# One layer of a pooling and sparse-attention trunk: the first gates computed as block products with seven multiplications

## The chip, the cores and the metric

The kernel runs on one core of a Trainium2 chip. A core has five engines with a queue each: PE (TensorE) multiplies matrices into PSUM, DVE (VectorE) and ACT (ScalarE) do elementwise work on SBUF and PSUM, POOL (GpSimd) does elementwise work on SBUF alone, and SP (SyncE) issues most DMAs. An engine works through its own queue in order and waits on semaphores for the others. The metric is the device time of one execution in microseconds (us). Before the change three runs gave 812.95, 813.62 and 814.96 us, median 813.62.

## The reference, cut to what matters

One layer (DEPTH = 1) on 512 tokens of width 1024, all in float32:

```python
h = rms_norm(x, norm_mix[l])
proj = h @ w_in[l]
u, q, kc, vc, ksl, vsl, kwn, vwn, g_nsa, g_merge = jnp.split(proj, IN_SPLITS, axis=-1)
y_pool = pool_mixer(u, w_pool[l], pool_scale[l])
y_nsa = nsa_mixer(q, kc, vc, ksl, vsl, kwn, vwn, g_nsa, ...)
g_a, g_b = jnp.split(jax.nn.sigmoid(g_merge), 2, axis=-1)
merged = g_a * (y_pool @ w_proj_pool[l]) + g_b * (y_nsa @ w_proj_nsa[l])
x = x + merged @ w_out[l]
h = rms_norm(x, norm_mlp[l])
x = x + jnp.square(jax.nn.relu(h @ w_ff1[l])) @ w_ff2[l]
return rms_norm(x, norm_final)
```

The change concerns `g_a`, "the first gates": columns 2352 to 3375 of `w_in` (1024 columns, in a projection of 1024 inputs by 512 tokens), and their sigmoid.

## The kernel before, in words

**Precision.** PE reads its operands in a reduced float32 (`FR`). Each float32 operand is therefore split into a high part (a copy rounded to `FR`, made by ACT) and a low part (the value minus the high part, made by DVE or POOL), and a product is made of three matmuls: high by high, high by low, low by high (`split_products`, line 396). The tokens' halves are `R1` and `R2` (`hT`), features on partitions, eight blocks of 128 by 512 tokens. A weight tile of 1024 columns is loaded by SP into one of four buffers with the tag "raw" (`emit_load`, line 216) and split by `emit_prep_half` (line 321, in two halves of 512) or `group_steps` (line 289, whole). Split weights go to a ring of two buffers ("wh", "wl"); some keys have a place of their own in `dest`, as the compression weights `wk`, `wv` have in `wkt`.

**Stages.** First the norm: rows of `x` are scaled and turned in four blocks of 128 tokens, and their halves written to `R1` and `R2` (`sums0`, `turn0`, `evac0`, lines 534 to 560). Then P1 (list at line 125, loop from line 853): all projections that must stand before the attention starts, in the order of the list. `fm` (line 462) makes one block of 128 output columns for all 512 tokens: 24 matmuls of 512 columns (eight k blocks by three), then a "post" step evacuates the PSUM bank. P1 makes the keys (`ck`, `ks`, `kw`), the values (`V0` to `V2`), the pooling inputs (`u0` to `u3`, mixed by `pool_mix` on DVE, line 790), the compression of keys and values (`wk`, `wv`, lines 707 and 722), the first three query blocks (`q0` to `q2`, with `rope`, line 612), the eight blocks of first gates (`ga0` to `ga7`, line 869: a sigmoid into `MA`), four small pooling products (`pool_out`, line 839), and the pooling projection (`pp0` to `pp3`, line 875), which multiplies `MA`. Stage P2 runs the attention with the remaining projections (`FILL2`: the second gates `gb` and `q3` to `q7`) as filler; then come the output projection and the MLP.

**The seven-product algorithm.** The MLP already uses it (class `Group`, line 1362, and `product`, line 1344). A weight of 1024 by 512 is taken as four blocks of 512 by 256, the input as four blocks of 512 features by 256 tokens. In place of eight block products it makes seven, of sums and differences of blocks: `A11`, `S3`, `S1`, `S2`, `A12`, `A22`, `S4`. A product is 24 matmuls of 256 columns. The sums of weight blocks are made on DVE or by DMA, the sums of tokens (`T1` to `T4`) on DVE, and each sum is split into high and low again. The results are put together in PSUM and on DVE (`main`, `last`): `A12` adds to the bank of `A11`, `A22` to that of `S3` after DVE has read it, `S4` to that of `S1` after DVE has read it (`NEEDS`).

**Places.** `GB` (4096 columns of float32) is the second gates' place in P2 and scratch in P1 (`cmp_first`, `pool_mix`). `oT` is the attention's output in P2 and scratch in P1 (`pool_mix`, `cmp_rest`, small weights). `MA` holds the first gates and is unused until `ga0`.

**Order.** The program text sets which work follows which by generators ("side") and by `ahead`, which prepares weights up to three keys ahead. The order in which instructions stand in each engine's queue is then fixed by the framework's scheduler when the program is built; it moves independent instructions past each other.

Of the kernel before, what the change touches and what calls it, by code (L numbers as in the profile page):

```python
# [62 lines left out]
def trunk(ctx: ExitStack, tc: tile.TileContext, A, out):  # L63
# [22 lines left out]
    GB = cp.tile([128, 8, S], F32, name="GB")  # L86
    GBf = GB.rearrange("p j t -> p (j t)")

# [16 lines left out]
    def add_key(k):  # L105
# [14 lines left out]
        else:  # L120
# [4 lines left out]
    P1 = ("ck ks u0 wk0 wk1 u1 wk2 u2 kw wk3 cv V0 V1 V2 wv0 u3 wv1 q0 wv2 wpool ga0 ga1 wv3 ga2 q1 "  # L125
          "ga3 ga4 ga5 q2 ga6 ga7 pp0 pp1 pp2 pp3").split()
    FILL2 = "gb0 q3 q4 q5 gb1 gb2 q6 gb3 q7 gb4 gb5 gb6 gb7".split()
    for k in P1 + FILL2:
        add_key(k)
# [8 lines left out]
    IN_TURN = ("A11", "S3", "S1", "S2", "A12", "A22", "S4")  # L138
# [77 lines left out]
    def emit_load():  # L216
# [22 lines left out]
        if i >= len(P1) + len(FILL2) + 4 and (len(begun) > 2 or begun and st["sums"] == len(jobs)):  # L239
            add_sum()  # L240
        return True

    def sums_after(i):

        if i < MLP0:
            return len(P1) + 3 <= i < len(P1) + len(FILL2) + 8
        return i % 3 == 0
# [72 lines left out]

    def emit_prep_half():
# [4 lines left out]
        if WL[i][0][0] in "AS":  # L326
            if "gen" not in part:
                part["gen"] = group_steps(i)
# [97 lines left out]

    hT = (R1, R2)
# [52 lines left out]
    oT = op.tile([128, 8, S], F32, name="oT")  # L480
    oTf = oT.rearrange("p j t -> p (j t)")
# [10 lines left out]
    rows = oTf[0:36, 2080:2208]  # L492
    w2 = {kv: oTf[:, 2208 + 128 * i:2336 + 128 * i].rearrange("p (k c) -> p k c", k=2) for i, kv in enumerate("kv")}
# [174 lines left out]
    with ExitStack() as c1:  # L668
# [9 lines left out]
        for k in P1:  # L678
            if k[:2] in ("wk", "wv"):
                dest[k] = wkt + ["wkt"]  # L680

        def cmp_first(kv):

            def post(ps):
                kc = GBf[:, 0:1024].rearrange("p (g t) -> p g t", g=2)
# [3 lines left out]
                a = GBf[:, 1024:2048].rearrange("p (j n) -> p j n", j=16)  # L689
# [32 lines left out]
        def cmp_rest(kv, ps):  # L722
            t = oTf[0:64, 1056:2080].rearrange("p (a n) -> p a n", a=4)
# [27 lines left out]
            pm = ps1.tile([128, 2, 64], F32, tag="M", bufs=2, name="psM")  # L751
            if kv == "k":
# [31 lines left out]
        POOL.memset(GBf[:, 2560:2576], 0.0)  # L784
        POOL.memset(GBf[:, 3088:3104], 0.0)
        yd = [p1.tile([128, 4, S], FR, name=f"yd{e}") for e in range(2)]

        mixing = []

        def pool_mix(g):  # L790
            def post(ps):
# [3 lines left out]
                u = oTf[:, 528 * (g % 2):528 * (g % 2) + 528]  # L795
# [5 lines left out]
                while sh < w:  # L801
                    nx = GBf[:, 2560 + 528 * (sh % 3 - 1):2560 + 528 * (sh % 3)]
# [4 lines left out]
                d = GBf[:, 2048:2560]  # L807
# [6 lines left out]
                mixing.clear()  # L814
            return post
# [30 lines left out]

        first_posts += [cmp_first("k"), lambda ps: rope(ps, -0.125, k_done(0))]
# [5 lines left out]
        for k in P1[2:]:  # L853
            i = int(k[-1]) if k[-1].isdigit() else None
            if k == "kw":
# [28 lines left out]
    OT = hT  # L884

# [4 lines left out]
    with ExitStack() as c2:  # L890
# [27 lines left out]
        def split_ready():  # L918

            while free and ready:  # L920
                p, half = ready.pop(0)
                c = slice(256 * half, 256 * half + 256)
                ACT.activation(OT[0][:, p, c], oT[:, p, c], AF.Copy)
                DVE.tensor_tensor(OT[1][:, p, c], oT[:, p, c], OT[0][:, p, c].bitcast(F32), op=ALU.subtract)
# [189 lines left out]
        def o_evac(p, half):  # L1114
# [3 lines left out]
            for h in range(2):  # L1118
                DVE.tensor_tensor(oT[64 * h:64 * h + 64, p, 256 * half:256 * half + 256].rearrange(
# [116 lines left out]
    MAf = MA.rearrange("p j t -> p (j t)")  # L1236

    def quarter(f, i):
        return f[:, 1024 * i:1024 * i + 1024].rearrange("p (k t) -> p k t", k=4)

# [96 lines left out]
    def pair(f, i):  # L1337
        return f[:, 512 * i:512 * i + 512]

# [3 lines left out]

    def product(ps, key, first, mm):

        w, n = use(key), 0
        for f in range(2):
            for k in range(4):
                for u, v in ((0, 0), (0, 1), (1, 0)):
                    mm(ps[:, 256 * f:256 * f + 256], w, f, k, u, v, start=first and n == 0, stop=n == 23,  # L1350
                       skip_group_check=True)
                    n += 1
                    if n % 6 == 0:
                        ahead()
                        step_side()

    def until(ready):
        while not ready():
            assert side
            step_side()  # L1360

    class Group:

        def __init__(self, c, g, Y):
            self.c, self.g, self.Y = c, g, Y
            self.s = pair(GBf, 6 + g)
            self.u2, self.u3, self.c21 = pair(MAf, 6 + g), pair(MAf, 0), pair(MAf, 1)
            self.ps, self.done = {}, set()  # L1370

        def pe(self, o):
            key = f"{o}1{self.c}{self.g}"
            until(lambda: o not in self.NEEDS or self.NEEDS[o] in self.done)
            if not self.done:
                side.append(self.main())
            name, x, *at = self.X[o]

            def mm(out, w, f, k, u, v, **kw):
                PE.matmul(out, w[u][:, k, 128 * f:128 * f + 128], XB[x][v][:, k, :], **kw)  # L1380
            if not at:
                self.ps[name] = bank()
# [270 lines left out]
```

## Time and profile before

| | us |
|---|---|
| three runs | 812.95, 813.62, 814.96 |
| the profiled execution's own time | 811.65 |
| its span | 809.8 |
| busy: PE, DVE, ACT, POOL | 788.0, 621.4, 491.3, 207.9 |
| first `fm` of P1 after the keys (`u0`) starts | 26.1 |
| last `pp` result multiplied | 170.1 |

The mean granted PE clock is 0.996 of full speed. The span is the time from the first to the last instruction on the core, the execution's own time adds what lies around it. In the rows, an instruction's duration includes its latency, so that matmuls and DVE instructions that follow each other without a wait overlap a little: the distance from start to start is what one costs in a queue that is never empty.

### The profile page before, as it was taken

To read this page: it belongs to the slowest core of one execution; us is meant where nothing else is said; L and a number is where in the kernel's file an instruction comes from. 1 tells how busy PE (TensorE), PEld (TensorE's weight loads), DVE (VectorE), ACT (ScalarE), POOL (GpSimd) and SP (SyncE) were. 2 spreads that over 40 slices of the span, in tenths; PEclk is the share of its full clock that TensorE was granted. 3 is DMA by queue.
4 is the path that set the end of the run, shared out by engine and by line. 5 is a ranking of instruction groups with operands and counts; after the bars stand their busy time and mean duration, and the time that the engine had idled before them with its cause. 6 is when DMAs were issued, how large, how long until landed. Compare 5 with 4: busy or idle time off the path is not lost.

```text
span 809.8 us, 14149 instructions
## 1 busy us (share of the span) xinstructions
PE 788.0 (97%) x5163; PEld 709.1 (88%) x5163; DVE 621.4 (77%) x1217; ACT 491.3 (61%) x968; POOL 207.9 (26%) x273
## 2 busy tenths in 40 slices
PE   8999999998999999999999999999999999999996
PEld 7889878887788888888788899999999999999996
DVE  5796744547888888888664579996899689978975
ACT  6576533327878788899434476934773477347833
POOL 4000000028777867674334100111111110000000
PEclk9999999999999999999999999999999999999999
DMA  9554632357456524554954807999899997754522
GB/s 306 141 161 120 167 92 92 104 162 164 66 134 136 129 72 93 104 132 93 313 146 155 203 2 217 317 242 284 243 285 225 286 262 207 211 165 156 185 76 105
DMA packets 128752, 136.65 MB, mean 169 GB/s; under 512 B 5349, under 2 KB 117001, under 8 KB 128522
## 3 DMA queue, kind: packets, MB, share of 16 engines
q1 hardware_dynamic: 107274, 113.98, 43.3%
q0 software_dynamic: 21120, 20.97, 18.2%
q8 instruction: 41, 0.67, 0.3%
q10 hardware_dynamic: 288, 0.79, 0.3%
q14 instruction: 29, 0.24, 0.1%
HBM read 131.01 MB, written 44.04 MB: 216 GB/s over the span
## 4 chain that ended last, share of the span: by engine, by line
PE 75%; DVE 14%; ACT 5%; issue 3%; POOL 2%; DMA 1%; SPq 0%; ACTq 0%; DVEq 0%; POOLq 0%
PE psF L394 22%; PE psB L1380 15%; PE psB L394 12%; PE psB L1499 9%; PE psO L1110 3%; PE psT L1076 3%; PE psS L1014 3%; DVE wl L308 2%; PE psV L394 2%; PE psF L451 1%; DVE w3l L308 1%; PE psC L714 1%; DVE P L1036 1%; ACT wh L306 1%; POOL P L1059 1%
## 5 line engine op out<-in xcount | busy, mean ns | idle before, releaser
L394 PE MATMUL psF<-R,wh 128*128 128x512 f32 x512 | 166.6, 404 | 0.8 <-ACT GB L688 0.6
L306 ACT ACTIVATE wh<-raw 128x1024 fp32r<-128x1024 f32 x70 | 74.0, 1058 | 74.0 <-PE psB L1499 32.6
L351 ACT ACTIVATE wh<-raw 128x512 fp32r<-128x512 f32 (+1 forms) x100 | 60.1, 620 | 82.5 <-PE psF L394 38.2
L394 PEld LDWEIGHTS psF<-R,wh 128*128 128x128 f32 x512 | 92.4, 189 | 19.0 <-ACT GB L688 0.9
L273 POOL DMA_DIRECT2D S<-w_ff x40 | 46.4, 1160 | 233.1 <-DMA S<-w_ff 163.5
L394 PE MATMUL psF<-R,wl 128*128 128x512 f32 x256 | 101.9, 398 | 0.4 <-DVE wl L353 0.4
L308 DVE TENSOR_TENSOR wl<-raw,wh 128x1024 fp32r<-128x1024 f32 x70 | 85.3, 1219 | 16.8 <-ACT wh L306 16.7
L1059 POOL TENSOR_SCALAR P<-P,sm,GT 128x128 f32<-128x128 f32 (+3 forms) x128 | 86.0, 708 | 42.2 <-DVE sm L1056 28.7
L353 DVE TENSOR_TENSOR wl<-raw,wh 128x512 fp32r<-128x512 f32 (+1 forms) x74 | 53.5, 734 | 33.3 <-ACT wh L351 32.3
L1046 ACT ACTIVATE P<-P,sm 128x128 f32<-128x128 f32 (+3 forms) x128 | 71.0, 556 | 9.5 <-DVE sm L1036 8.5
L1036 DVE CUSTOM_DVE_ANT_0 P<-psS,cst 128x128 f32<-128x128 f32 (+3 forms) x128 | 59.7, 484 | 6.8 <-PE psT L1076 5.1
L1380 PE MATMUL psB<-R,wh 128*128 128x256 f32 x352 | 64.1, 282 | 0.0
L1087 ACT ACTIVATE PT<-psT 128x512 fp32r<-128x512 f32 (+2 forms) x96 | 49.5, 520 | 19.7 <-PE psT L1076 19.0
L353 POOL TENSOR_TENSOR wl<-raw,wh 128x512 fp32r<-128x512 f32 x28 | 38.1, 1364 | 88.4 <-ACT wh L351 86.1
L306 ACT ACTIVATE w3h<-raw 128x1024 fp32r<-128x1024 f32 x35 | 37.0, 1056 | 39.2 <-PE psB L1499 17.0
L1091 DVE TENSOR_TENSOR PT<-psT,PT 128x512 fp32r<-128x512 f32 (+2 forms) x96 | 56.5, 594 | 3.4 <-ACT PT L1087 2.6
L394 PEld LDWEIGHTS psF<-R,wl 128*128 128x128 f32 x256 | 48.3, 189 | 11.4 <-DVE wl L353 0.6
L1076 PE MATMUL psT<-ident,P 128*128 128x128 f32 x320 | 51.6, 275 | 4.8 <-POOL P L1059 4.0
L1380 PEld LDWEIGHTS psB<-R,wh 128*128 128x128 f32 x352 | 54.1, 189 | 0.3 <-DVE R L1322 0.2
L308 DVE TENSOR_TENSOR w3l<-raw,w3h 128x1024 fp32r<-128x1024 f32 x35 | 42.7, 1220 | 14.4 <-ACT w3h L306 14.4
L1076 PEld LDWEIGHTS psT<-ident,P 128*128 128x128 f32 x320 | 40.0, 142 | 14.7 <-POOL P L1059 6.9
L1380 PE MATMUL psB<-R,wl 128*128 128x256 f32 x176 | 49.5, 281 | 0.0
(385 smaller groups left out, 2295.7 us busy)
## 6 DMA issues: line engine op xcount, KB each, us to landing
raw<-w_ff SPq DMA_DIRECT2D x55, 512.0 KB, 5.2
S<-w_ff POOLq DMA_DIRECT2D x40, 512.0 KB, 7.7
raw<-S SPq DMA_DIRECT2D x40, 512.0 KB, 4.4
raw<-w_in SPq DMA_DIRECT2D x32, 512.0 KB, 3.9
S<-w_ff SPq DMA_DIRECT2D x30, 512.0 KB, 5.4
S<-S SPq DMA_DIRECT2D x10, 512.0 KB, 6.2
raw<-w_proj_nsa SPq DMA_DIRECT2D x8, 512.0 KB, 4.2
raw<-w_out SPq DMA_DIRECT2D x8, 512.0 KB, 3.5
```

The lines of the kernel that those rows point to most:

```text
L306: ACT.activation(h, t, AF.Copy)
L308: DVE.tensor_tensor(l, t, h.bitcast(F32), op=ALU.subtract)
L351: ACT.activation(h[:, sl], t[:, sl], AF.Copy)
L353: eng.tensor_tensor(l[:, sl], t[:, sl], h[:, sl].bitcast(F32), op=ALU.subtract)
L394: PE.matmul(ps, a, b, start=first and j == 0, stop=last and j == n - 1, skip_group_check=True)
L1036: DVE.tensor_tensor_reduce(out=P[:, o:o + n].rearrange("p (a c) -> p a c", c=128), in0=s, in1=m, scale=1.0, scalar=3e38, op0=ALU.add, op1= ...
L1046: last_exp[:] = [ACT.activation(c, c, AF.Exp, bias=sm[:, 0, e:e + 1], scale=-1.0, accum_out=sm[:, 1, e:e + 1])]
L1059: r = POOL.tensor_scalar(P[:, o:o + n], P[:, o:o + n], sm[:, 2, e:e + 1], GT[:, qb, c + e:c + e + 1], op0=ALU.mult, op1=ALU.mult)
L1076: PE.transpose(pt[:, 128 * j:128 * j + 128], P[:, 128 * j:128 * j + 128], ident)
L1091: DVE.tensor_tensor(dL, src, dH.bitcast(F32), op=ALU.subtract)
L1380: PE.matmul(out, w[u][:, k, 128 * f:128 * f + 128], XB[x][v][:, k, :], **kw)
L1499: PE.matmul(out, YB[y][u][:, k, 128 * f:128 * f + 128], w[v][:, k, :], **kw)
```

## The change

The eight blocks `ga0` to `ga7` (8 by 24 matmuls of 512 columns) become two groups `GA0` and `GA1` of 512 gate columns each, every group made by the class `Group` with seven products of 24 matmuls of 256 columns. `product`, `until` and `Group` move up in the file and take their bank, operands and places as arguments; the MLP calls them with the old ones.

- *Weights*: per group four blocks of 512 by 256 are loaded into the four "raw" buffers (`add_gates`), and their sums made in place by DVE (`gate_steps`). Each of the fourteen operands is split whole (1024 columns). `S1` and `A22` use the place of the compression weights (`wkt`), the other five the ring.
- *Tokens*: `token_sums` adds the halves of `R1` and `R2` back to float32 in `MA`, makes `T1` to `T4` on DVE, and splits each. `T3` and `T1` lie in the place of `GB`, once pooling's four mixings no longer use it as scratch, `T2` and `T4` in the two halves of the place of `oT`.
- *Order of P1*: `q0` and `q1` move ahead of the gates, `u3` behind `q0`, all four `wv` and `wpool` ahead of `GA0`; `q2` stands between the groups. The four `pool_out` stand behind the first four products of `GA0`.
- `GB` and `oT` are allocated after P1 in the same places; `oT` in two tiles.

```diff
-    P1 = ("ck ks u0 wk0 wk1 u1 wk2 u2 kw wk3 cv V0 V1 V2 wv0 u3 wv1 q0 wv2 wpool ga0 ga1 wv3 ga2 q1 "
-          "ga3 ga4 ga5 q2 ga6 ga7 pp0 pp1 pp2 pp3").split()
+    P1 = ("ck ks u0 wk0 wk1 u1 wk2 u2 kw wk3 cv V0 V1 V2 wv0 q0 wv1 u3 wv2 q1 wv3 wpool GA0 q2 GA1 "
+          "pp0 pp1 pp2 pp3").split()
...
+    def add_gates(g):
+        at = {b: len(LD) + n for n, b in enumerate(("21", "11", "22", "12"))}
+        for b in at:
+            i, j, c = int(b[0]) - 1, int(b[1]) - 1, 2352 + 512 * g
+            w = w_in[512 * j:512 * j + 512, c + 256 * i:c + 256 * i + 256]
+            LD.append([(w.rearrange("(k p) c -> p k c", p=128), 0)])
+        gate_loads.append(at)
+        WL.extend((f"{o}G{g}", None) for o in IN_TURN)
...
+    def gate_steps(i):
+        o, g = WL[i][0][:-2], int(WL[i][0][-1])
+        if o == "A11":
+            kept.clear()
+        for b in {"A11": ("11",), "S3": ("21",), "S1": ("22",), "A12": ("12",)}.get(o, ()):
+            while st["load"] <= gate_loads[g][b]:
+                assert emit_load()
+            kept[b] = raws.pop(gate_loads[g][b])[0]
+        h, l = dest[WL[i][0]][:2] if WL[i][0] in dest else slot_of(i)
+        to, b = {"S3": ("11", "21"), "S1": ("21", "22"), "S2": ("11", "22")}.get(o, ("12" if o == "S4" else o[1:], None))
+        t = kept[to]
+        if b:
+            DVE.tensor_tensor(t, t, kept[b], op=ALU.add)
+            yield
+        ACT.activation(h, t, AF.Copy)
+        yield
+        DVE.tensor_tensor(l, t, h.bitcast(F32), op=ALU.subtract)
...
+        if o == "A12":
+            yield
+            DVE.tensor_tensor(t, t, kept["11"], op=ALU.add)
+        if o in ("S1", "A12", "A22", "S4"):
+            emit_load()
...
+        def token_sums():
...
+            def sum_of(o, to, a=None, b=None, alu=None):
+                if alu:
+                    DVE.tensor_tensor(to, a, b, op=alu)
+                    yield
+                if o == "T3":
+                    made[:] = flat(cp.tile([128, 8, S], FR, tag="GB", bufs=1, name="TS"))
+                elif o != "T1":
+                    made[:] = flat(op.tile([128, 4, S], FR, tag=f"oT{o == 'T2':d}", bufs=1, name="TS"))
+                h, l = (made.pop(0) for _ in range(2))
+                ACT.activation(h, to, AF.Copy)
+                yield
+                DVE.tensor_tensor(l, to, h.bitcast(F32), op=ALU.subtract)
...
+            for b in ("11", "12", "22", "21"):
+                whole(b)
+                yield
+            while len(mixed) < 4:
+                yield
+            DVE.tensor_tensor(x["11"], x["11"], x["12"], op=ALU.subtract)
+            yield from sum_of("T3", x["12"], x["22"], x["12"], ALU.subtract)
+            yield from sum_of("T1", x["11"])
+            yield from sum_of("T2", x["11"], x["22"], x["11"], ALU.add)
...
+            yield from sum_of("T4", x["21"], x["11"], x["21"], ALU.subtract)
...
-            elif k[:2] == "ga":
-                def post(ps, j=i):
-                    ACT.activation(MA[:, j, :], ps, AF.Sigmoid)
-                run(fm(k, ps1, post))
-                if i < 4:
-                    pool_out(i)
+            elif k[:2] == "GA":
...
+                group = gates(i)
+                for n, o in enumerate(IN_TURN):
+                    group.pe(o)
+                    if i == 0 and n < 4:
+                        pool_out(n)
```

`Group`'s steps on DVE, as in the MLP:

```python
DVE.tensor_tensor(self.u2, self.s, self.ps["b"], op=ALU.subtract)
DVE.tensor_tensor(self.u3, self.ps["c"], self.u2, op=ALU.add)
self.done.add("u3")
yield
DVE.tensor_tensor(self.u3, self.ps["d"], self.u3, op=ALU.add)
self.done.add("u2")
```

More of the change, by code (lines that the diff above doesn't have):

```diff
@@ new lines, in gates, with act @@
+        def gates(g):
+            def act(src, f, th):
+                yield
+                ACT.activation(MA[:, 4 * g + 2 * f:4 * g + 2 * f + 2, 256 * th:256 * th + 256],
+                               src.rearrange("p (f t) -> p f t", f=2), AF.Sigmoid, scale=-1.0 if f else 1.0)
+            own = [pair(gate_f[0], i) for i in range(4)]
+            at = own[1:] + own[:1] if g else [own[0], pair(MAf, 6), pair(MAf, 7), pair(MAf, 4)]
+            return Group(f"G{g}", sums_of.get, lambda: ps1.tile([128, S], F32, tag="V", bufs=4, name="psV"), at, act)
```

218 lines of the change are left out of this document (128 added, 90 removed).

## The prediction

> **What bounds the kernel now.** I began with the page: the busy times, and the chain that ended last.
>
> ```profile
> span 809.8 us, 14149 instructions
> PE 788.0 (97%) x5163; PEld 709.1 (88%) x5163; DVE 621.4 (77%) x1217; ACT 491.3 (61%) x968; POOL 207.9 (26%) x273
> PE 75%; DVE 14%; ACT 5%; issue 3%; POOL 2%; DMA 1%; SPq 0%; ACTq 0%; DVEq 0%; POOLq 0%
> ```
>
> PE is the bound over the whole, DVE the second. What a change in P1 is worth has to be read in P1, so I asked for the busy time by stretches (columns: length, then PE, weight load, DVE, ACT, POOL busy, the granted clock, DMA).
>
> ```profile
> 20.00:40.00 20.00, 19.35 (x116) 16.81 (x115) 15.29 (x27) 11.63 (x22) 0.16 (x1) 1.00 0.50 140
> 40.00:60.00 20.00, 20.00 (x99) 16.73 (x98) 18.07 (x40) 13.97 (x27) 0.00 (x0) 1.00 0.59 168
> 60.00:86.00 26.00, 26.00 (x159) 23.59 (x158) 19.23 (x39) 15.01 (x34) 0.00 (x0) 1.00 0.47 130
> 86.00:127.00 41.00, 40.80 (x185) 32.61 (x184) 24.32 (x52) 18.54 (x35) 1.39 (x4) 1.00 0.43 118
> 127.00:170.00 43.00, 43.00 (x189) 35.12 (x188) 18.12 (x31) 11.79 (x22) 0.29 (x1) 1.00 0.41 119
> 195.40:199.50 4.10, 4.10 (x19) 3.51 (x19) 2.46 (x11) 2.28 (x6) 2.65 (x4) 0.62 0.70 160
> ```
>
> From 40 to 170 us PE never stops. DVE is nearly full from 40 to 60 and about 60% and 42% busy in the stretches where the gates are made. So PE's work counts there, as long as DVE's stays below it. The last row is used further down. The chain in order of time gives PE's prices:
>
> ```profile
> 73.05 0.95 PE psC L714 x8
> 74.00 5.60 PE psF L394 x24
> 80.55 5.59 PE psF L394 x24
> 120.14 51.35 PE psF L394 x222
> 171.49 0.81 PE psC L950 x8
> ...
> 499.96 10.26 PE psB L1380 x86
> 540.27 17.38 PE psB L1499 x144
> ```
>
> A matmul of 512 columns costs 51.35/222 = 0.2313 us, one of 256 columns 10.26/86 = 0.1193 (0.1207 in the last row).
>
> **The saving on PE.** Removed are 8 x 24 = 192 matmuls of 512 columns: 44.4 us. Added are 14 x 24 = 336 of 256 columns: 40.1 us. The saving is 4.3 us (3.8 at the dearer price). A block product less in eight saves 12.5% of the columns, but the narrow matmul costs 3% more per column.
>
> **What DVE gets.** Prices, start to start in a full queue:
>
> ```profile
> 518.85 1.14 DVE wl L308
> 519.98 0.60 DVE yT3L L1439
> 537.17 1.22 DVE raw L317
> 538.39 1.13 DVE w3l L308
> ...
> 118.46 0.76 DVE L626 TENSOR_TENSOR rx<-rx,cst 128x256 f32<-128x256 f32 x2 [2.77 <-DMA rs<-rx]
> 119.14 0.76 DVE L629 TENSOR_TENSOR rs<-rs,cst 128x256 f32<-128x256 f32 x2
> 123.28 0.20 DVE L777 TENSOR_TENSOR VC<-psM,VC 32x64 fp32r<-32x64 f32 x1
> ```
>
> 1024 columns cost 1.14, 512 columns 0.60 to 0.69 (I take 0.62), 256 columns (119.14 - 118.46)/2 = 0.34, a tiny one 0.2. Removed are 16 subtractions of 512 columns, 9.9 us. Added are 14 subtractions and 8 weight sums of 1024 (25.1 us), four whole tokens, four sums and four subtractions of 1024 (13.7 us), and ten steps of the groups of 512 (6.2 us): 45.0 us, net 35 us more on DVE over P1. That would fit into P1's idle time if it were spread out. The changed program's queue shows that it isn't: the whole tokens and two sums are placed before 35 us, but the other two sums and all four splits need places that pooling's last mixing (`u3`) or the value compression still holds, and so stand behind `u3`.
>
> So I follow DVE's queue from there. In the old order the second full block after the values ends at 80.55 + 5.59 = 86.14; in the new one it is `u3`. With the start's delay of 0.4 (below) it ends at 86.5, ACT's copy takes 0.58:
>
> ```profile
> 80.61 0.58 ACT L797 ACTIVATE oT<-psF 128x512 f32<-128x512 f32 x1
> ```
>
> and DVE starts `u3`'s first running sum at 87.1. From it up to the step that frees the bank of `S1` for `S4` in the first group (the last of `main`) the queue holds, in its built order, 17 instructions of 1024 columns (four sums and seven low parts of weights; low parts of T3, T1, T2, T4 and the sums for T2 and T4), 19 of 512 (`wv3`'s two, `u3`'s six, four for `q0` and `q1`, four of `pool_out`, three of `main`), 13 of 256 (rope's adds and products, the GELU of the value compression), 10 tiny ones: 17 x 1.14 + 19 x 0.62 + 13 x 0.34 + 10 x 0.2 = 37.6 us, without a single wait. To the step before it that frees the bank of `S3` for `A22`: 35.8 us, so 122.9.
>
> PE's work from 86.5 to the start of `A22` is `wv2`, `q1`, `wv3` (0.95 + 5.59 + 0.95), five products (14.3), four `pool_out` (12 x 0.2313 = 2.8), 0.6 for the small compression products and 0.5 for two matmuls of `q2` that the new order puts there: 25.7, so PE would be there at 112.2. It waits 122.9 - 112.2 = 10.7 us, in pieces that the same count gives: `S3` wants the low part of `T3` at 98.2 and gets it after 14.0 us of the queue, at 101.1; `S1` wants its own low part and gets it at 106.0; `S2` at 112.5; `A12` ends at 118.2, `A22` starts at 122.9. Almost nothing that could fill these waits stands there: the queue has `q2`'s other 22 matmuls behind `S4`. Bounds: at 1.13 and 0.60 throughout, 1 us less; every wait of DVE itself adds, and ACT stands in the chain with a high part of 1.06 between sum and subtraction:
>
> ```profile
> L306 ACT ACTIVATE wh<-raw 128x1024 fp32r<-128x1024 f32 x70 | 74.0, 1058 | 74.0 <-PE psB L1499 32.6
> ```
>
> ACT has some 11 of these there plus 10 shorter ones, about 20 us in the same 36, so it delays, but isn't full. I keep 8.5 to 12.7.
>
> **The second group.** `q2`'s 22 matmuls (5.1 us) run while DVE makes `GA1`'s first operands. DVE's last step of the first group waits for `S4`, so its queue for `GA1` starts only there: that step, two low parts, three sums ahead of `S3`'s low part come to about 8.5 us after `S4` against PE's 5.1 + 2.86 = 8.0 for arriving at `S3`; and `A22` waits 0.4 more behind the rope of `q2` and the `S4` sum. I take 0.9, between 0 and 3. From there `pp` follows as before.
>
> **The start.** Two of the four whole tokens stand behind the first four subtractions of the turned tokens and ahead of the scaling of token blocks 2 and 3:
>
> ```profile
> 11.73 0.69 DVE L559 TENSOR_TENSOR R<-psTr,R 128x512 fp32r<-128x512 f32 x1 [0.23 <-ACT R L557]
> 13.09 0.16 DVE L538 RECIPROCAL r<-r 128x1 f32<-128x1 f32 x1 [0.67 <-ACT r L537]
> 14.80 1.41 DVE L541 SCALAR_TENSOR_TENSOR x<-x,r,psM 128x512 f32<-128x512 f32 x2
> 18.23 1.29 DVE L559 TENSOR_TENSOR R<-psTr,R 128x512 fp32r<-128x512 f32 x2 [0.82 <-ACT R L557]
> ...
> 19.59 4.16 PE psF L451 x34
> ```
>
> 12.42 + 2 x 1.14 = 14.7, then two scalings with their reciprocals end at 17.85 in place of 16.21: 1.6 us late. PE's second half of the first keys started at 19.59 and needs the low halves; four subtractions of 0.64 from 17.9 bring the first three at 19.9. So 0.4 us, between 0 and 1.6. The four later ones fall into DVE's gaps between 20 and 35 us (4.7 idle in the first row of stretches): the operands of `u0`, `wk0`, `u1` still come 1 us ahead of PE by the same kind of count; without that cover they cost up to 1 us.
>
> **Loads.** Eight of 512 KB stay eight; the four "raw" buffers are now held until a group's sums are done, so `GA1`'s third load is issued when `S4`'s low part is made (124 us) and lands about 4 us later:
>
> ```profile
> raw<-w_in SPq DMA_DIRECT2D x32, 512.0 KB, 3.9
> ```
>
> DVE wants it at about 132. Behind these loads SP's queue holds `q2`'s rope copies, wanted later still. I cost it at nothing, covered by those 4 us.
>
> **The clock.** Where PE idles, its clock can fall. The one place in the old trace is the seam to the attention:
>
> ```profile
> 190.32 0.39 PE L394 MATMUL psF<-R,wl 128*128 128x512 f32 x1
> 192.93 0.44 PE L1076 MATMUL psT<-ident,P 128*128 128x128 f32 x2 [2.21 <-POOL P L1059]
> 193.94 0.44 PE L1076 MATMUL psT<-ident,P 128*128 128x128 f32 x2 [0.58 <-POOL P L1059]
> ```
>
> After these 2.8 us of idle the clock was 0.62 over 4.1 us (last row of the stretches): 0.38 x 4.1 = 1.6 us lost. The new waits, 3 us before `S3` and nearly 5 before `A22`, are as long; what is lost ahead of a product that DVE holds up anyway costs nothing, after `A22` it costs all. I take 1.0, between 0 and 1.7.
>
> The Trainium skill ("TensorE: Matmul & The Clock Gate", Part 1: The HAM clock gate) says that the clock goes to half after an idle window of about 3.4 us and returns after about as much sustained work; the windows run freely. By that rule only the wait before `A22` is sure to count, with an estimated 3.4 x 0.5 = 1.7 us, and the sum would be 0.7 higher. The trace agrees with the length and shows that two idle pieces of 2.21 and 0.58 us sufficed.
>
> **The sum.** Against the profiled execution's 811.65 us: -4.3 (PE) + 0.4 (start) + 10.7 (first group) + 0.9 (second) + 1.0 (clock) = +8.7, so 820.4. That execution lies 1.97 below the median of the runs, 813.62; the median I expect at 822.3, rounded 822. P2 and what follows keep their instructions and order on PE and POOL and stay bound as they are, so the delay passes through: the chain goes from the last `pp` into the attention's first scores (the row at 171.49). Its own range: all lower bounds give 813.6 - 4.3 + 8.5 = 818, all upper ones 813.6 - 3.8 + 2.6 + 12.7 + 3 + 1.7 = 829.8; not all at once, so 817 to 828.
>
> **The rivals.**
>
> *DVE is hidden.* If DVE's queue keeps ahead of PE, PE's saving stands alone: 813.6 - 4.3 + 0.4 = 809.7. For it speaks that DVE was 60% busy from 86 to 127 and that PE is the bound of the whole; against it, that the 37.6 us of DVE between `u3` and `S4` are counted at prices of a full queue, while PE has 28.6 us there. It decides as soon as the count is wrong by 9 us. Chance 0.10.
>
> *Savings and waits cancel.* If DVE is half as late (some of the counted instructions done ahead of `u3`, or the seam's own 2.8 us of idle and 1.6 of clock gone because DVE and ACT enter P2 with less left over), 813 to 816. Against: the queue's order is fixed, and the seam's wait is on POOL, whose instructions don't change. Chance 0.07.
>
> *The clock falls at every wait.* Each wait of the first group and the one in `GA1` puts PE on half speed; PE, not DVE, then becomes late for `A22`, from the point where two slow products in a row (2 x 2.86 more) outlast DVE's lead of 4.7 us. Three dips of 1.6 in place of 1.0: 826 to 829. For it speaks the seam; against, that DVE has up to 4.7 us in hand to hide the slow products. Chance 0.08.
>
> The forecast keeps 0.75. **How the numbers follow.** To leave out no more than 2 in 10 the range takes in the forecast's own range and most of the cancelling case and the slow clock: 813 to 828. About 0.3%, 2.4 us, is what a measurement of this kernel can tell from no change. Faster: the hidden case, 0.10. Same (811.2 to 816.1): the cancelling case and a little of the forecast's low end, 0.08. Slower: the rest, 0.82.
>
> **What would show it.** Between about 87 and 125 us the changed profile should show DVE busy nearly all the time and PE with waits on DVE before the second matmul of `S3` (the low part of `T3`), before `S1`, `S2` and `A22`, together about 10 us, and a granted clock below 1 shortly after. The last multiplication by `MA` should end near 178 in place of 170, and the attention and the MLP be as long as before. It is wrong if PE stays full there, if the waits name a DMA or ACT, or if the later stages change their length.

## The result, and the profile after

| | median of 4 runs, us | lowest to highest | profiled execution | its span |
|---|---|---|---|---|
| before | 814.29 | 812.95 to 815.04 | 811.65 | 809.8 |
| after | 825.98 | 824.44 to 828.32 | 826.01 | 824.2 |

The change makes the kernel slower: the ratio is 1.0153, with a 95% interval of 1.0134 to 1.0173, 11.7 us between the medians. The forecast was 822, with a range of 813 to 828: the median lies inside the range, 4 us above the forecast, and the longest of the four runs (828.32) just outside. The two profiled executions lie 14.4 us apart.

From the page of the changed kernel, the span, the busy times and the chain that ended last:

```profile
span 824.2 us, 14477 instructions
PE 789.1 (96%) x5307; PEld 717.0 (87%) x5307; DVE 654.7 (79%) x1245; ACT 501.8 (61%) x972; POOL 206.7 (25%) x273
PE 65%; DVE 20%; ACT 7%; issue 4%; POOL 2%; DMA 2%; ACTq 0%; DVEq 0%; POOLq 0%
```

PE is busy for as long as before (789.1 against 788.0), with 144 matmuls more; DVE works 33.3 us more (654.7 - 621.4; the prediction counted 35). In the chain PE's share falls from 75 to 65%, and DVE's rises from 14 to 20%. The stretches of P1 (length, then PE, weight load, DVE, ACT, POOL busy, granted clock, DMA):

```profile
60.00:86.50 26.50, 26.50 (x165) 24.27 (x164) 18.03 (x38) 16.30 (x35) 0.00 (x0) 1.00 0.45 121
98.00:130.00 32.00, 22.94 (x136) 19.99 (x135) 30.23 (x47) 17.14 (x24) 1.17 (x4) 0.85 0.28 73
130.00:155.00 25.00, 23.95 (x174) 22.60 (x174) 18.59 (x23) 11.30 (x15) 0.00 (x0) 0.98 0.27 79
155.00:182.00 27.00, 27.00 (x143) 23.30 (x142) 13.51 (x21) 7.32 (x13) 0.00 (x0) 1.00 0.54 152
```

Up to 86.5 us PE is full. From 98 to 130, where the first group is made, DVE is the full engine (30.23 of 32) and PE has 9 us of idle time, at a clock of 0.85. What PE waited for between 60 and 155 us (sum, times, longest):

```profile
PE psV L512 <- DVE MA L533: 3.3, 1, 3.3
PE psV L512 <- ACT TS L1003: 2.2, 1, 2.2
PE psF L443 <- ACT wh L400: 1.6, 1, 1.6
PE psV L512 <- DVE TS L1005: 1.1, 1, 1.1
PE psV L512 <- DVE gs L533: 1.1, 1, 1.1
```

The token sum T3 (`TS`, its high part on ACT and its low part on DVE) holds `S3` for 3.3 us. The weights of `q2` and the step of `main` that frees the bank of `S3` (`MA L533`) hold PE for 4.9 us ahead of `A22` (1.6 + 3.3). The last row is the same step in the second group. Small stretches around these waits show the clock:

```profile
103.70:107.10 3.40, 3.40 (x18) 3.40 (x18) 3.40 (x7) 0.57 (x2) 0.00 (x0) 0.52 0.00 0
120.60:124.00 3.40, 0.74 (x2) 0.30 (x2) 3.25 (x7) 1.55 (x4) 0.67 (x3) 1.00 0.78 190
124.00:130.90 6.90, 5.15 (x24) 5.15 (x25) 4.54 (x8) 0.63 (x1) 0.42 (x2) 0.51 0.58 151
130.90:134.30 3.40, 3.40 (x29) 3.31 (x29) 0.97 (x2) 0.98 (x2) 0.00 (x0) 1.00 0.35 120
```

The granted clock falls to half at each long wait, for 3.4 us the first time and 6.9 us the second; all 24 matmuls of `A22` lie in the second dip. Of the chain, the first matmuls of the attention's compressed scores and the first long piece of the MLP's output products:

```profile
183.79 0.81 PE psC L1143 x8
...
553.93 17.38 PE psB L1611 x144
```

Before, they stood at 171.49 and 540.27: 12.3 us are lost up to the first row, 13.7 up to the second, 14.4 up to the end. Not all of it is the change's. PE's first matmul waits for a load that the change doesn't touch; before:

```profile
2.27 3.75 PE L522 MATMUL psM<-grow,ones 1*128 1x512 f32 x4 [2.27 <-DMA grow<-norm_mix]
```

and after:

```profile
3.38 3.75 PE L645 MATMUL psM<-grow,ones 1*128 1x512 f32 x4 [3.38 <-DMA grow<-norm_mix]
```

So P1 is compared from PE's first matmul to the first `psC` row: 171.49 - 2.27 = 169.2 us before, 183.79 - 3.38 = 180.4 after, 11.2 more.

### The profile page after: what moved, and what is told of

Its sections match the earlier page's. It is cut to its first block, busy times and chain, and to the rows that moved or that the text cites. A ratio compares the mean times of both kernels' runs of the same rounds, so it can differ in the third digit from the quotient of the medians.

```text
span 824.2 us, 14477 instructions
## 1 busy us (share of the span) xinstructions
PE 789.1 (96%) x5307; PEld 717.0 (87%) x5307; DVE 654.7 (79%) x1245; ACT 501.8 (61%) x972; POOL 206.7 (25%) x273
## 4 chain that ended last, share of the span: by engine, by line
PE 65%; DVE 20%; ACT 7%; issue 4%; POOL 2%; DMA 2%; ACTq 0%; DVEq 0%; POOLq 0%
PE psF L443 15%; PE psB L443 12%; PE psB L512 12%; PE psB L1611 9%; PE psO L1303 3%; PE psT L1269 3%; PE psV L512 3%; DVE wl L330 3%; PE psS L1207 3%; PE psV L443 2%; DMA raw<-w_ff 1%; DVE w3l L330 1%; POOL P L1252 1%; DVE P L1229 1%; PE psC L840 1%
## 5 line engine op out<-in xcount | busy, mean ns | idle before, releaser
L443 PE MATMUL psF<-R,wh 128*128 128x512 f32 x384 | 126.0, 406 | 2.3 <-ACT wh L400 1.6
L400 ACT ACTIVATE wh<-raw 128x512 fp32r<-128x512 f32 (+1 forms) x84 | 49.5, 617 | 54.6 <-PE psF L443 22.2
L443 PEld LDWEIGHTS psF<-R,wh 128*128 128x128 f32 x384 | 68.5, 189 | 14.5 <-ACT wh L400 1.8
L443 PE MATMUL psF<-R,wl 128*128 128x512 f32 x192 | 76.5, 398 | 0.4 <-DVE wl L402 0.4
L402 DVE TENSOR_TENSOR wl<-raw,wh 128x512 fp32r<-128x512 f32 (+2 forms) x58 | 42.3, 746 | 15.3 <-ACT wh L400 14.2
L1303 PE MATMUL psO<-PT,VV 128*128 128x256 f32 x320 | 48.6, 286 | 0.0
```

Of the source, the lines that this page charges most:

```text
L402: eng.tensor_tensor(l[:, sl], t[:, sl], h[:, sl].bitcast(F32), op=ALU.subtract)
L443: PE.matmul(ps, a, b, start=first and j == 0, stop=last and j == n - 1, skip_group_check=True)
L1303: PE.matmul(ps[:, qb % 2, :, :], VV[:, k, b, g, :], t[:, j, :, :], start=False, stop=last and j == len(kbs) - 1 and t is tL, skip_group_ch ...
```

## The experiments

**My theory**: the first group waits for DVE's queue behind `u3` (token sums, weight sums and low parts in a row), and the half-speed clock after the longest wait adds to it. **The rivals**: the weights themselves (their loads, their high parts on ACT) come late; the narrow products or the new order cost time of their own; it is the amount of DVE's work, not its place. All runs in one table; P1 is the length just defined, "old" is the old kernel on the same chip.

| run | time, us | old, us | PE's first matmul | first psC | P1 | against P1 of e1 |
|---|---|---|---|---|---|---|
| before, profiled | 811.65 | | 2.27 | 171.49 | 169.2 | -10.3 |
| after, profiled | 826.01 | | 3.38 | 183.79 | 180.4 | +0.9 |
| e1, changed kernel again | 822.39 | 814.02 | 2.38 | 181.86 | 179.5 | 0 |
| e2, no token sums | 814.58 | 814.02 | 3.33 | 174.00 | 170.7 | -8.8 |
| e3, no weight sums | 815.83 | 814.02 | 2.33 | 174.89 | 172.6 | -6.9 |
| e4, PE kept warm | 821.63 | 814.02 | 2.29 | 179.91 | 177.6 | -1.9 |
| e5, neither kind of sums | 808.51 | 811.93 | 2.30 | 167.46 | 165.2 | -14.3 |
| e6, u3 earlier | 821.43 | 811.93 | 2.28 | 180.02 | 177.7 | -1.7 |
| e7, sums on POOL | 834.54 | 811.93 | 3.43 | 192.84 | 189.4 | +9.9 |
| e8, both | 832.22 | 811.93 | 2.42 | 191.96 | 189.5 | +10.1 |
| e9, sums spread | 821.40 | 813.37 | 2.35 | 178.71 | 176.4 | -3.1 |
| e10, spread, u3 earlier | 819.65 | 813.37 | 2.29 | 177.08 | 174.8 | -4.7 |
| e11, and pool_out later | 818.29 | 813.37 | 3.50 | 177.92 | 174.4 | -5.1 |
| e12, one group only | 813.21 | 811.92 | 2.38 | 173.27 | 170.9 | -8.6 |

e1 to e5 are single runs, the times of the others medians of 4 runs (e12: 11); PE's first matmul, the first psC row and P1 always come from one profiled execution. The wait for the norm row goes from 2.27 to 3.50 us, and is 3.38 and 2.38 for the same kernel (after, e1), so it is chance. What follows the first psC row is left out of P1 because it moves as well: in the fourteen profiles it takes 637.2 to 640.6 us, and 640.4 and 638.7 for the same kernel.

**e1: the changed kernel again**, no edit.

> The changed kernel once more, unchanged, to see what its profiled execution shows by chance. In the first one the start waited 3.4 us for the norm row in place of 2.3, and the MLP had a wait of 7.7 us on a w_ff load near 507 us, which together with slower stretches there made 2.5 us of the 14.4 between the two profiles. Theory (both are chance): here the start wait and the MLP's length differ from the first profile by 0.5 to 3 us, while the stretch from the second full block after the values to the first psC matmul of the attention keeps its length (87.56 to 183.79, 96.2 us) to within 0.5 us. Rival (the change causes them): 3.4 us at the start and the same MLP length within 0.3 us again.

It took 822.39 us, 3.6 less than the first profile. From its queue on PE and its chain:

```profile
2.38 3.75 PE L645 MATMUL psM<-grow,ones 1*128 1x512 f32 x4 [2.38 <-DMA grow<-norm_mix]
```

```profile
181.86 0.81 PE psC L1143 x8
...
402.75 30.72 PE psB L443 x131
...
550.57 17.38 PE psB L1611 x144
```

Of the 3.6 us the start's wait makes 1.0, and the output projection with the MLP's first part 1.5 (550.57 - 402.75 = 147.8 us; 149.3 in the first profile, whose chain has 7.69 us of a load of w_ff there). P1 itself is 0.9 shorter, and its stretch from the second full block on 0.6, not within the 0.5 that was expected: in the first profile DVE waited 2.33 us for the copies of a rope just ahead of `u3`'s sums, here 1.69, and PE's wait on T3's high part is 0.6 shorter. So about 1 us of P1 is chance too. e1 is what the other runs are held against: P1 is 10.3 us longer than before, the rest of the span 0.4 (820.6 - 181.86 against 809.8 - 171.49). It is one run, and shorter than each of the four before it (824.44 to 828.32), so it stands at the low end of what the changed kernel takes.

**e2: no token sums.**

```
         def token_sums():
...
+            sums_of.update({"T1": parts["11"], "T2": parts["12"], "T3": parts["22"], "T4": parts["12"]})
+            yield
+            return
```

> The four whole tokens, the four token sums and the four low parts of sums are left out (12 instructions of 1024 columns on DVE and the high parts on ACT); the group products read plain token blocks instead, so the first gates come out as other numbers. PE's work is the same. Theory (PE waits for DVE's queue behind u3): 6 of the 17 instructions of 1024 columns go out of the queue between u3 and S4, 6.8 us; the waits before S3, S1 and S2 vanish and the wait before A22 falls from 3.3 to under 1.5 us; time 7 to 9 us under the changed kernel (817 to 819). Rival (PE waits for the weights, their loads, their high parts on ACT or the groups themselves): under 2 us less (824 to 826).

P1 falls by 8.8 us, against 6.8 for the instructions alone; of PE's waits the one on `MA L533` shrinks, and new small ones name the weights' high parts:

```profile
PE psV L512 <- ACT wkt L360: 1.3, 1, 1.3
...
PE psV L512 <- DVE MA L533: 0.8, 1, 0.8
```

`A22` runs at full speed here, which is worth another 2.1 us (below). The theory holds; 4.8 us of waits are left over P1's gates. But the four high parts of the token sums are gone from ACT too, so this run alone doesn't tell DVE's work from ACT's; the next one does.

**e3: no weight sums.**

```
         if b:
-            DVE.tensor_tensor(t, t, kept[b], op=ALU.add)
             yield
...
         if o == "A12":
             yield
-            DVE.tensor_tensor(t, t, kept["11"], op=ALU.add)
```

> The eight weight sums of the two groups are left out (8 instructions of 1024 columns on DVE, 4 in each group); the products S1 to S4 read plain weight blocks instead, so the first gates come out as other numbers. PE's, ACT's and the loads' work is the same. Theory (DVE's queue): 4 x 1.14 = 4.6 us out of the first group's queue and the 1.1 us wait of the second group gone: 4.6 to 6 us under the changed kernel (820 to 821.5). Rival (what PE waits for comes late whatever DVE does, by loads or ACT): within 1 us of the changed kernel.

P1 falls by 6.9 us, a little more than expected: the four sums in the first group's queue count for 4.6, and the dip of the clock ahead of `A22` is gone, as PE's row for `A22` shows (5.40 us in e1, below):

```profile
120.59 3.14 PE L510 MATMUL psV<-TS,wkt 128*128 128x256 f32 x24 [1.65 <-DVE MA L531]
```

Loads and high parts are the same as in the changed kernel, so the rival that names them falls.

**e5: neither token nor weight sums** (the edits of e2 and e3 together).

> Both the token part (four whole tokens, four sums, four low parts) and the eight weight sums are left out, so the seven products of a group run on plain blocks and the first gates come out as other numbers. What is left of the change is PE's 336 matmuls of 256 columns in place of 192 of 512, in the new order. Theory (the saving of 4.3 us on PE is real, and only DVE's sums eat it): no wait on DVE behind u3 over 0.5 us in either group, the first psC matmul of the attention 3 to 4.5 us sooner after PE's first matmul than in the old kernel (169.2 us there), time 809 to 811 (with 1 us of chance in the start's wait). Rival (the narrow products are slower, or the order and the loads cost something of their own): the first psC matmul no sooner than in the old kernel, time 813 to 815.

P1 takes 165.2 us, 4.1 less than in the old kernel; its one wait of more than 0.1 us is 0.9 on a product of the compression. The time, one run, is 3.4 us under the median of the old kernel on the same chip. So the saving on PE is real, and the narrow products and the new order cost nothing that shows beside 1 us of chance. The two kinds of sums, with the high parts of the token sums on ACT, cost 14.3 us together. Where they are lost shows in the first matmuls of `A11` and of `A22`, in PE's order of time; e5:

```profile
93.58 0.40 PE L510 MATMUL psV<-R,wh 128*128 128x256 f32 x2
...
112.61 3.00 PE L510 MATMUL psV<-R,wkt 128*128 128x256 f32 x24
115.73 0.48 PE L510 MATMUL psV<-R,wh 128*128 128x256 f32 x2
```

and e1:

```profile
93.53 0.40 PE L512 MATMUL psV<-R,wh 128*128 128x256 f32 x2
...
123.81 5.40 PE L512 MATMUL psV<-TS,wkt 128*128 128x256 f32 x24 [3.33 <-DVE MA L533]
129.05 0.40 PE L512 MATMUL psV<-R,wh 128*128 128x256 f32 x2
```

From `A11` to `A22` e1 needs 30.3 us, e5 19.0: 11.3 more, of which 0.5 are two matmuls of `q2` that stand there in e1. `A22` itself takes 5.2 in place of 3.1.

**e4: PE kept warm.**

```
         w, n = use(key), 0
+        if key == "A22G0":
+            junk = ps1.tile([128, 256], F32, tag="M", bufs=2, name="psM")
+            for j in range(36):
+                PE.matmul(junk, w[0][:, j % 4, 0:128], sums_of["T4"][0][:, j % 4, :], start=True, stop=True,
+                          skip_group_check=True)
```

> 36 extra matmuls of 256 columns, whose result nothing reads, are put on PE between A12 and the next two matmuls of q2, ahead of A22 of the first group, where PE waits for DVE anyway (36 x 0.12 = 4.3 us at full clock; 3.3 + 1.6 us of wait were there). Theory (the wait before A22 halves the clock and A22 pays): A22 and S4 take 5.7 to 6.2 us in place of 8.2, the time falls by 1.5 to 2.5 us (823.5 to 824.5) as the extra work fits into the wait. Rival (A22 is slow for its own reasons, or the clock was already down and falls whatever PE does there): A22 keeps 5 us, and the extra work adds 0 to 4 us.

PE's rows, the extra work and `A22`:

```profile
118.33 4.46 PE L482 MATMUL psM<-TS,wkt 128*128 128x256 f32 x36
...
124.13 3.14 PE L517 MATMUL psV<-TS,wkt 128*128 128x256 f32 x24 [0.86 <-DVE MA L538]
```

With 4.5 us of work that nobody needs in the wait, `A22` takes 3.1 us in place of 5.2, and P1 gets 1.9 shorter. The half-speed clock ahead of `A22` is shown to be a cost of its own, about 2 us. The time moved by less than 1 us against e1 (821.63, 822.39), as the later parts were 1.1 us longer in this execution.

**e6: u3 earlier.**

```
-    P1 = ("ck ks u0 wk0 wk1 u1 wk2 u2 kw wk3 cv V0 V1 V2 wv0 q0 wv1 u3 wv2 q1 wv3 wpool GA0 q2 GA1 "
+    P1 = ("ck ks u0 wk0 wk1 u1 wk2 u2 kw wk3 cv V0 V1 V2 u3 wv0 q0 wv1 q1 wv2 wv3 wpool GA0 q2 GA1 "
...
-            if k[:2] in ("wk", "wv"):
+            if k[:2] in ("wk", "wv") and k != "wv3":
...
             elif k[0] == "q":
+                while scored["rope"]:
+                    step_side()
```

> Only the order of P1 is changed: u3 goes ahead of wv0 and q0, so that DVE can start on its queue behind u3 some 13 us sooner, and wv3 moves behind wv2; every instruction stays. Theory (DVE's queue behind u3 sets the end of the first group; PE has 13 us more of other work to run beside it): the wait before A22 and those before S3, S1 and S2 fall from about 10 us to 0 to 4, no dip of the clock in A22, time 7 to 11 us under the changed kernel (812 to 818, against 822 to 826). Rival (the amount of DVE's work in P1 is the bound whatever the order, or new waits for u3's operands or the rope's copies come in): under 3 us less.

Ratio to the old kernel 1.0126 (1.0106 to 1.0145), P1 only 1.7 us shorter than in e1: the rival was right. Its stretches:

```profile
60.00:80.00 20.00, 20.00 (x131) 18.66 (x130) 13.93 (x29) 13.24 (x29) 0.00 (x0) 1.00 0.45 132
80.00:98.00 18.00, 15.23 (x80) 12.57 (x78) 17.47 (x30) 11.86 (x20) 0.00 (x0) 1.00 0.49 147
98.00:125.00 27.00, 23.84 (x141) 21.36 (x142) 26.52 (x43) 13.62 (x20) 1.17 (x4) 0.81 0.25 71
```

DVE is full from 80 to 125 us all the same. With `u3` the splits and ropes of `wv2`, `q1` and `wv3` came into the queue, and the 6 us that DVE idles between 60 and 80 us stayed idle. A product that brought its own vector work along covered little here.

**e7: the sums on POOL**, and **e8: on POOL, with u3 earlier.**

```
-            DVE.tensor_tensor(t, t, kept[b], op=ALU.add)
+            POOL.tensor_tensor(t, t, kept[b], op=ALU.add)
...
-                    DVE.tensor_tensor(to, a, b, op=alu)
+                    POOL.tensor_tensor(to, a, b, op=alu)
```

> The eight weight sums and the four token sums of 1024 columns are made on POOL in place of DVE; the order stays. In the queue behind u3 DVE loses two token sums and four weight sums, 6 x 1.14 = 6.8 us. POOL's price for 1024 columns is not in the trace; two instructions of 512 there take 1.36 us each, so about 2.7. Theory (DVE's queue alone): waits before A22 and the others fall by 6 to 7 us and the clock's 2.3 comes back, less what the longer sums add to the chain sum, high part, low part (1.6 us each, where nothing else is in the way): time 4 to 8 us under the changed kernel (815 to 820). Rival (POOL slows DVE down beside it, or the sums' own latency sets the chain): within 3 us of the changed kernel.

> Both edits: u3 ahead of wv0 and q0, and the sums on POOL. Theory: DVE's queue behind u3 is some 31 us and starts 13 us sooner, so it ends before PE wants A22; what is left is PE's saving of 4.3 us less the start's 0.4: 809 to 812, at or under the old kernel (813.6). Rival (the sums on POOL come late, or the new order has waits of its own): 814 or more.

Ratios 1.0284 (1.0259 to 1.0308) and 1.0249 (1.0233 to 1.0265): P1 grows by 10 us in both. POOL's queue in e7:

```profile
95.02 5.70 POOL L358 TENSOR_TENSOR raw<-raw,raw 128x1024 f32<-128x1024 f32 x2 [59.86 <-DMA raw<-w_in]
...
114.33 5.25 POOL L996 TENSOR_TENSOR MA<-MA 128x1024 f32<-128x1024 f32 x2 [8.79 <-DVE TS L1005]
```

and DVE's beside it:

```profile
94.97 0.68 DVE L785 TENSOR_TENSOR Q<-rx,Q 64x512 fp32r<-64x512 f32 x1
95.68 2.78 DVE L931 TENSOR_TENSOR scratch<-scratch 128x520 f32<-128x520 f32 x1
98.50 2.77 DVE L787 TENSOR_TENSOR Q<-rx,Q 64x512 fp32r<-64x512 f32 x1
101.29 0.69 DVE L936 SCALAR_TENSOR_TENSOR scratch<-scratch,ea 128x512 f32<-128x512 f32 x1
...
114.78 0.74 DVE L973 SCALAR_TENSOR_TENSOR yd<-psF,pec,yd 128x512 fp32r<-128x512 f32 x1
117.97 2.69 DVE L362 TENSOR_TENSOR wl<-raw,wh 128x1024 fp32r<-128x1024 f32 x1 [2.45 <-ACT wh L360]
```

A sum takes POOL 2.6 to 2.9 us in these rows (2.3 to 3.3 in e7), and while it runs a DVE instruction with two operands in SBUF stands still: 2.78 us for what costs 0.7 otherwise, 2.69 in place of 1.2. So DVE doesn't win the 1.14 us of a sum, it loses up to 2.1. The instruction that reads one operand from PSUM (`psF`, 0.74) went on beside POOL. The Trainium skill ("SBUF — State Buffer", SBUF: two separate sides) says the same: the pair of ports that DVE and GpSimd share is locked for a whole instruction, against DVE instructions with two SBUF inputs. The trace agrees. The delay reaches PE by way of `T3`: its high part starts at 107.70 us, 98.41 in e1, as its place comes free with `u3`'s last step on DVE, and PE waits 5.8 us for it ahead of `S3`. How much of the 10 us is the lock, and how much the longer chain of sum, high part and low part, is not shown. The rivals were right, but e7 loses far more than the 3 us that its rival allowed.

**e9: the sums spread.** The sums for T2 and T4 are made in the places of the whole tokens, and T3 and T2 get places that are free earlier (GB is split into two halves).

```
-            while len(mixed) < 4:
-                yield
             DVE.tensor_tensor(x["11"], x["11"], x["12"], op=ALU.subtract)
...
+            DVE.tensor_tensor(x["12"], x["22"], x["12"], op=ALU.subtract)
+            yield
+            with behind(cA["low"]):
+                DVE.tensor_tensor(x["22"], x["22"], x["11"], op=ALU.add)
+                DVE.tensor_tensor(x["21"], x["22"], x["21"], op=ALU.subtract)
+            yield
+            yield from sum_of("T3", x["12"])
+            yield from sum_of("T2", x["22"])
+            while len(mixed) < 4:
+                yield
+            yield from sum_of("T1", x["11"])
```

> The token sums keep their number, but do not wait for u3 any more: the places of GB are given as two halves, the sums for T2 and T4 are made in the places of the whole tokens, and those two sums and the splits of T3 (first half of GB) and T2 (oT1) are let in as soon as the turned rows of cv are split, near 60 us, where DVE had 6 us of idle time in 20. Behind u3 only the low parts of T1 and T4 are left: 4 x 1.14 = 4.6 us less in the queue of the first group. The order of P1's products stays. Theory (it is the pile behind u3, not the amount of DVE's work): 4.6 us and, as the wait before A22 gets short, the clock's 2.3 us come back: 5 to 7 us under the changed kernel, ratio to the old kernel 1.006 to 1.010. Rival (the amount counts, DVE has no room near 60 us): under 2 us, ratio 1.013 or more.

Ratio 1.0100 (1.0083 to 1.0117), P1 3.1 us shorter. The stretch where the work went, and `A22`:

```profile
60.00:80.00 20.00, 20.00 (x132) 18.67 (x130) 17.41 (x33) 13.99 (x29) 0.00 (x0) 1.00 0.36 106
```

```profile
120.91 5.15 PE L512 MATMUL psV<-TS,wkt 128*128 128x256 f32 x24 [3.60 <-DVE MA L533]
```

DVE took 17.41 of 20 us from 60 to 80 (13.44 in e1), and PE stayed full there: the room was real. The ratio is at the upper end of what the theory gave, P1's 3.1 us lie between the two accounts: the wait ahead of `A22` stayed, and the dip with it.

**e10: spread, with u3 earlier**, the edits of e9 and e6, and **e11: the same with `pool_out` in the second group** (`if i == 0 and n < 4` becomes `if i == 1 and n < 4`).

> The spread sums and the order with u3 ahead of wv0 and q0 together. Theory: both gains add, 2.5 us of the order and 5 to 7 of the sums: ratio to the old kernel 1.002 to 1.007. Rival (they use the same idle time of DVE near 60 to 80 us, and so do not add): ratio as with the spread sums alone.

> As the kernel with both, and the four pool_out products with their DVE steps (4 x 0.75 = 3.0 us) go from the first group into the second, where DVE was busy 18.4 of 25 us. Theory (DVE's queue up to A22 sets the end of the first group): 2 to 3 us under the kernel with both, ratio to the old kernel 0.998 to 1.004. Rival (PE loses 2.8 us of work that filled its waits, and the second group, with its own wait of 1.1 us, gets what the first loses): within 1 us of the kernel with both.

Ratios 1.0077 (1.0059 to 1.0094) and 1.0061 (1.0043 to 1.0080): the gains of e6 and e9 nearly add in P1 (1.7 + 3.1 against 4.7), though the ratio is just above what was expected; `pool_out` gives another 0.4 in P1 (1.4 between the medians) in place of 2 to 3, nearer to its rival. What PE waits for in e11:

```profile
PE psV L512 <- ACT wh L360: 2.3, 3, 1.2
PE psF L443 <- ACT wh L400: 1.3, 2, 0.7
```

No wait names `MA L533` any more, as in e10; what is late now are high parts on ACT behind sums on DVE. Relieved of the queue, the group waits for the chain sum, high part, low part.

**e12: one group only.** The first four gate blocks as in the old kernel, the second group by the seven products, with the sums of e9.

```
-    P1 = ("... V0 V1 V2 wv0 q0 wv1 u3 wv2 q1 wv3 wpool GA0 q2 GA1 "
+    P1 = ("... V0 V1 V2 wv0 u3 wv1 q0 wv2 wpool ga0 ga1 wv3 ga2 q1 ga3 q2 GA1 "
```

> Only the second group of 512 columns is made by the seven products; the first four gate blocks are made as in the old kernel, in the old order of P1, and the token sums are spread as in the kernel with spread sums. PE saves half: 96 x 0.2313 - 168 x 0.1193 = 2.2 us. DVE gets some 20 us more than in the old kernel between 0 and 160 us, but nothing of a group behind u3, and 120 to 150 us, where the old kernel's DVE was 40% busy, is free for the second group. Theory (the seven products pay where DVE has room): -2.2 + 0.4 (start) + 1.1 (the second group's own wait): 0 to 2 us under the old kernel, ratio 0.997 to 1.000. Rival (any group makes PE wait for its sums, wherever it stands): the wait and clock of the second group grow to 3 us or more, ratio 1.002 or more.

Ratio 1.0014 (1.0004 to 1.0024), about 1 us slower than the old kernel. PE's waits:

```profile
PE psV L512 <- DVE wl L362: 1.5, 1, 1.5
PE psV L512 <- DVE gs L533: 0.8, 1, 0.8
PE psV L512 <- ACT wkt L360: 0.5, 1, 0.5
```

2.8 us of waits in the second group against the 1.1 expected, which eat the 2.2 saved; the clock doesn't fall in P1 here. The result lies between the two accounts, nearer to the rival's: a group makes PE wait here too, where DVE's share of the stretch was 42% before. No version that computes the real gates beats the old kernel; e12 is the nearest.

## Why the prediction was right, and where it was off

The forecast, slower by about 8.7 us through DVE's queue behind `u3`, came true by its mechanism; e1 measures +10.3 in P1. The median of the first four runs lies 11.7 us above the old kernel's, 3 more than forecast, and by the time alone 825.98 lies nearer to the slow-clock rival (826 to 829) than to the forecast's 822; it is the traces that decide. Term by term:

- **The saving on PE**, -4.3: e5 shows -4.1, with a wait of 0.9 in it. Right, to within the 1 us by which P1 moves.
- **The start**, +0.4: from PE's first matmul to `u0` the three profiles have 23.84 us before, 24.18 after, 23.78 in e1. At most 0.3.
- **The first group**, +10.7: e1 against e5 gives 11.3 - 0.5 = 10.8. The queue was counted well; its dates in e1:

```profile
86.87 0.71 DVE L931 TENSOR_TENSOR scratch<-ea 128x527 f32<-128x527 f32 x1
...
99.77 1.21 DVE L1005 TENSOR_TENSOR TS<-MA,TS 128x1024 fp32r<-128x1024 f32 x1
...
104.71 1.21 DVE L362 TENSOR_TENSOR wkt<-raw,wkt 128x1024 fp32r<-128x1024 f32 x1
...
111.39 1.23 DVE L362 TENSOR_TENSOR wl<-raw,wh 128x1024 fp32r<-128x1024 f32 x1
...
123.06 0.69 DVE L533 TENSOR_TENSOR MA<-psV,MA 128x512 f32<-128x512 f32 x1
```

  Predicted were a start at 87.1, the low part of T3 at 101.1 (101.0 here), that of `S1` at 106.0 (105.9), that of `S2` at 112.5 (112.6), and `A22` at 122.9 (123.8). Not all of the 10.8 is seen as idle time: the first dip of the clock made PE slow for 3.4 us ahead of products that DVE held up anyway, so part of the wait there is slow work: around `S1` and `S2` the rows show only 0.9 us of idle time, where the prediction's count leaves some 3 (10.7 less 2.9 ahead of `S3` and 4.7 ahead of `A22`). That it would cost nothing beyond was said, and holds, as DVE has no gap from 86.87 to 123.06. Two of PE's waits in the first profile, 2.2 and 1.6 us, name ACT, which the prediction had called a sign of being wrong. Both stand behind DVE: in e1 the high part of `T3` starts at 98.41, when `u3`'s last step on DVE has ended (98.18), and the weights of `q2` come in ACT's queue behind the high part of `T4`, for whose sum ACT waits 3.07 us.
- **The second group**, +0.9: from `A11`'s first matmul to `pp0` e1 takes 21.5 us and e5 19.9, so 1.6; the wait on `gs L533` is 1.0 of it, the rest isn't located.
- **The clock**, +1.0, between 0 and 1.7: this term was mis-sized. e4 shows about 2, `A22` in e1 against e5 2.1. I took its price from the seam's 4.1 us at 0.62, as if the dip began with PE's work and lasted some 3.4 us. The dip ahead of `A22` lasts 6.9 us, with 5.2 of work in it. By the Trainium skill ("TensorE: Matmul & The Clock Gate", Part 1: The HAM clock gate) the clock comes back after a window of about 3.4 us of sustained work, in windows that run freely; 6.9 is two such windows, as if the first, in which PE was idle for 1.75 us, didn't count. The trace agrees with the length, and with the windows: read in steps of 0.1 us, e1's clock changes at 101.66, 105.08, 122.14, 128.97, 204.06 and 207.48 us, whole multiples of 3.41 us apart, and so it does in every other profile with more than one dip up to 215 us, from another starting point each time. What a window must hold is not shown: in e1 a half-speed window with 1.74 us of work was followed by another, in e6 one with 3.21 us too, but in e4 one with 3.02 us was not. So part of this term is luck: it depends on where a wait falls among the windows.
- **The loads**, at nothing: no wait of PE in the gates names one. But DVE's queue starts with a rope whose copies come by DMA, and the 0.6 us more that DVE waits for them in the first profile delayed the group; I had no term for that.
- **Beyond P1**, no change: +0.4 in e1, +2.1 in the first profile, most of it around loads of w_ff in the MLP that the change doesn't touch; such a load is in the chains of e9 to e12 again, and what brings it is not shown. In the first profile start, rope copies and MLP all came out long.

The sum for e1 is -4.1 + 10.8 + 1.6 + 2.1 = 10.4, against 10.3 measured. The rival "DVE is hidden" falls with e2 and e3, and "savings and waits cancel" (813 to 816) with the four runs, of which the shortest took 824.44; "the clock falls at every wait" was half right, with two dips in P1, of which only the second cost anything.

## What to carry to other kernels

A product saved by sums is paid on the engine that makes the sums: here 4 us of PE cost 33 us of DVE, and a count of that engine's queue, from the instruction that frees the places on, gave the first group's loss to within 1 us where its share of the span (77%) gave no hint of it. Work moved up ahead of such a queue helped little here, as it brought vector work along (e6), and sums spread into idle time helped until the next link, here ACT's high parts, was late (e9 to e11). A wait of PE can have a second price, the half-speed product after it: here 2.1 us after 4.9 us of waits.

## What was not expected of the hardware

- After a wait of 3.3 us (with 1.6 more just ahead) PE's granted clock was 0.5 for 6.9 us; after waits of 2.2 and 1.1 us, for 3.4. Between 60 and 215 us the clock of each profile changes only at whole multiples of 3.41 us from its first change there. The 24 matmuls of 256 columns took 5.2 us in place of 3.1.
- In e7 POOL's sum of 1024 columns (2.3 to 3.3 us) stops DVE's instructions with two SBUF operands for its whole length: 2.78 us for a sum of 520 columns that takes 0.70. An instruction with one operand in PSUM ran beside it at 0.74.
- A kernel's time on one core moved by 3.6 us between two profiled executions of the same program, through the first load (2.38, 3.38), a rope's copies and loads in the MLP.
